# A hybrid decoder layer on one core: the attention's step as two blocks of both heads

## Chip, core and metric

The kernel runs on one NeuronCore of a Trainium2 chip. The metric is the device time of one execution in microseconds (us). An interval or a median is over several executions.

## What is computed

The layer takes `x` of 1024 tokens by 1024 features (float32). Two attentions read projections of the same modulated input: A, a sliding window of 128 tokens with 16 query heads on 2 key heads and a sink logit for each head, and B, three dilations (1, 4, 16) of 8 heads each, joined by the softmax of their log-sums. A feed-forward block follows. Cut to what matters here:

```python
s = jnp.einsum('nbqhgd,nbkhd->nbhgqk', qb, kw, preferred_element_type=jnp.float32) * (dh ** -0.5)
s = jnp.where(mask[None, :, None, None], s, NEG_INF)
m = jnp.max(s, axis=-1)                       # A: also against the sink
p = jnp.exp(s - m[..., None])
denom = jnp.sum(p, axis=-1)                   # A: plus exp(sink - m)
o = jnp.einsum('nbhgqk,nbkhd->nbqhgd', p, vw.astype(jnp.float32))
o = o / denom_t[..., None]
...
merged = jax.nn.sigmoid(ga) * ya + jax.nn.sigmoid(gb) * yb
x = layer_norm(DEEPNORM_ALPHA * x + (1.0 + gate_m) * y, ln1_g[l], ln1_b[l])
```

A block is 128 queries; it sees its own 128 keys and, where the pattern asks for it, the 128 before. A head has 64 features.

## The kernel before

Every float32 product is made of parts: an operand is split into a leading part (`hi`, in a format that TensorE (PE) multiplies in one pass) and the rest (`lo`), and three products are summed: hi*hi, hi*lo, lo*hi. For the weights that is `mac` (lines 130 to 133), for the scores it is done by stacking. A head has only 64 features, so `q_stacks` puts q_hi and q_lo of one head on the two halves of the 128 rows (partitions), and `k_stacks` puts k_hi on both halves: one product of 128 rows gives q_hi*k_hi + q_lo*k_hi. The rest, q_hi*k_lo, is a product of 64 rows. It lies on rows 0 to 63 (`LO`) for head 0 of a pair and on rows 64 to 127 (`HI`) for head 1.

**Units and steps.** A unit is one pair of heads: 12 units of B (4 pairs by 3 dilations), then 8 of A. Each unit has 8 blocks for each of its heads. All blocks but the first see the block before in B's first dilation and in A (products of 256 columns, the first of 128); every other block does in the second dilation; none does in the third. The list `subs` (line 723) cuts a unit into four steps: half 0 with head 0, half 0 with head 1, half 1 with head 0, half 1 with head 1, where a half is four blocks. So a step has four 128-row products (`s<-kh,qs`), then four 64-row products (`s<-kl,qs`), all of one head, all on line 497. They fill two banks of the accumulator (PSUM), two blocks in each; the pool `ps_s` has just these two.

**The rest of a step.** VectorE (DVE) reads each block's scores, scales and masks them into `probs` and takes the maximum (`mx`, line 505); two blocks' maxima are negated into `st` (line 510 or 513). ScalarE (ACT) takes exponentials (line 519). One step later `turn_probs` transposes the blocks on PE into banks `pt` (line 535) and ScalarE copies them to `ptsb` (line 536). After the two steps of a half, `weigh` makes the sums of the values (`po`, line 556), the two heads on the two halves of the output columns.

**What sets the order.** Each engine runs its instructions in program order (`manual_schedule`). The projections are a generator, `stream`, in pieces of six matmuls (a tick); the loop over the steps pumps a number of ticks (`at`) between its parts, so that attention is woven into the projections. A unit of B and the first of A have 24 ticks, the other A units 8. The projections run ahead of the attention by `LEAD = 6` ticks. A unit's query stacks are made two and three ticks behind their projection, head 0 first (`soon`), each by a copy on ScalarE (line 432) and a subtraction on VectorE (line 433). POOL does a part of the rotation; SP issues nearly all DMAs, POOL those of the last A pair's end.

Of the kernel before, what the change touches and what calls it, by code (L numbers as in the profile page):

```python
# [40 lines left out]
class Weights:  # L41
    """Streams weights in pieces of 512 columns: DMA, an optional scale, and two exact parts."""
# [15 lines left out]
    def step(self):  # L58
        """Splits the next piece and sends for the one that fits behind it."""
# [17 lines left out]
    def prepare(self, pieces):  # L77
        """Sees to it that the next pieces are split."""
        while len(self.done) < min(self.used + pieces, len(self.jobs)):
            self.step()  # L80

    def take(self, pieces):
        """The next pieces, as a function from the chunk to its two parts."""
        self.prepare(pieces)
        got = self.done[self.used:self.used + pieces]
        self.used += pieces
        kh = got[0][2]
        n = 512 // kh
        return lambda k: [got[k // kh][s][:, (k % kh) * n:(k % kh + 1) * n] for s in range(2)]
# [3 lines left out]
def decoder_layer(ctx: ExitStack, tc: tile.TileContext, I, out, dbg=None):  # L93
# [20 lines left out]
    # silu(c), one value per partition and chunk of the contraction  # L114
# [6 lines left out]
    def wide(name, pool, halves=(0, 1)):  # L121
        """A [128, 8, 1024] array in two exact parts: a function of part, token half and chunk."""
# [87 lines left out]
    early = {}  # L210
    with tc.tile_pool(name="pro", bufs=2) as pro:
# [52 lines left out]
        def first_macs(j):  # L264
            """What the j-th chunk of u^T brings to the first projections, in pieces."""
# [18 lines left out]
        def table_steps():  # L284
            """The rope's angles, reduced to [-pi, pi] (cosines as sines of a quarter turn less the angle's size)."""
# [141 lines left out]
    def q_stacks(e, r, box):  # L427
        """Per head [q_hi; q_lo], the leading part on the head's own partitions."""
# [13 lines left out]
    def k_stacks(e, r, both, box):  # L442
        """Per head [k_hi; k_hi] and k_lo, on the head's own partitions or on both halves."""
# [21 lines left out]
    def values(e, r, box):  # L465
        """Values [key in block, block, feature], tokens in the order of their residue modulo r."""
# [17 lines left out]
    def scores(un, half, h):  # L484
        """Scaled and masked scores of four blocks of a head, and their maxima, negated."""
        own = (LO, HI)[h]
        box, prev, st = un["box"], un["prev"], un["st"]
        probs = att.tile([P, 4, 2, P], F32, name="probs", bufs=2)
        un["probs", half, h] = probs
        khs, kls = (box["kh"], box["kl"]) if "kv" not in un else ([kv_a["kh"][un["kv"]]] * 2, [kv_a["kl"][un["kv"]]] * 2)  # L490
        q = box["q"][h]
# [8 lines left out]
        mx = att.tile([P, 4], F32, name="mx", bufs=3)  # L500
        for i2 in range(2):
            for j in range(2):
                i = 2 * i2 + j
                lo = 0 if prev(4 * half + i) else 1
                nc.vector.tensor_tensor_reduce(
                    out=probs[:, i, lo:], in0=pss[i2][:, j, lo:], in1=un["mask"][:, lo:], scale=QS, scalar=NEG,
                    op0=OP.add, op1=OP.max, accum_out=mx[:, i:i + 1])
            sl = slice(4 * half + 2 * i2, 4 * half + 2 * i2 + 2)
            if "kv" in un:
                nc.vector.tensor_scalar(st[:, 0, h, sl], mx[:, 2 * i2:2 * i2 + 2], un["sink"](h), -1.0,  # L510
                                        op0=OP.max, op1=OP.mult)
            else:
                nc.vector.tensor_scalar(st[:, 0, h, sl], mx[:, 2 * i2:2 * i2 + 2], -1.0, None, op0=OP.mult)  # L513
    def exponentials(un, half, h):
        prev, st, probs = un["prev"], un["st"], un["probs", half, h]
        for i in range(4):
            b = 4 * half + i
            pr = probs[:, i, 0 if prev(b) else 1:]
            nc.scalar.activation(pr, pr, AF.Exp, bias=st[:, 0, h, b:b + 1], accum_out=st[:, 1, h, b:b + 1])  # L519
    def slots_of(un, half):  # L520
        slots = []
        for b in range(4 * half, 4 * half + 4):
# [5 lines left out]
    def turn_probs(un, half, h):  # L528
        probs, slots = un.pop(("probs", half, h)), slots_of(un, half)
        ptsb = att.tile([P, 8, P], F32, name="ptsb", bufs=3)  # L530
        for s0 in range(0, len(slots), 4):
            part = slots[s0:s0 + 4]
            pt = ps_t.tile([P, 4, P], F32, name="pt")
            for i, (b, kb) in enumerate(part):
                nc.tensor.transpose(pt[:, i, :], probs[:, b - 4 * half, int(kb == b)], ident)  # L535
            nc.scalar.activation(ptsb[:, s0:s0 + len(part), :], pt[:, :len(part), :], AF.Copy)
        un["pts", half, h] = ptsb

    def weigh(un, half):
        """Sums of the values for four blocks of both heads."""  # L540
        slots = slots_of(un, half)
# [7 lines left out]
        pts = [un.pop(("pts", half, h)) for h in range(2)]  # L549
# [3 lines left out]
        for ji, (kb, i, n, c0) in enumerate(jobs):  # L553
            for h in range(2):
                c = un["kv"] if "kv" in un else h
                nc.tensor.matmul(po[(LO, HI)[h], c0:c0 + n * P], v[:, kb, c * 64:(c + 1) * 64], pts[h][:, i:i + n, :],  # L556
# [20 lines left out]
    def keep_sums(un):  # L577
        """The reciprocal sums of A's exponentials, the sinks' among them."""
# [22 lines left out]
    def side(p):  # L601
        """The last pair's end keeps to the engine that has nothing else to do then."""
# [96 lines left out]
    def tasks(n, i):  # L699
        """What follows the attention of earlier units."""  # L700
# [22 lines left out]
    subs = [(un, half, h) for un in units for half in range(2) for h in range(2)]  # L723
    pump(ends[0] + LEAD + 2)
    for s in range(len(subs) + 2):
# [4 lines left out]
        if s < len(subs):  # L730
            un, half, h = subs[s]
            if half == 0 and h == 0:
                un["st"] = att.tile([P, 2, 2, NB], F32, name="st", bufs=3)
            scores(un, half, h)
# [6 lines left out]
        if s >= 2:  # L741
            un, half, h = subs[s - 2]
            if h == 1:
                weigh(un, half)
                if half == 1:
# [436 lines left out]
```

## Time and profile before

| | |
|---|---|
| time, median of 3 runs | 1977.31 us (1974.82 to 1979.35) |
| span of the profiled execution, first to last instruction | 1974.0 us |
| PE / DVE / ACT / POOL busy | 98% / 55% / 34% / 20% |
| attention and its projections | about 88 to 830 us |

The page gives no time of its own for the profiled execution beside its span; the median of the timed runs lies 3.3 us above that span. Matmuls are pipelined and their ends are modelled, so what a matmul costs is read from the distance between starts, not from its duration. `PEld` is the load of the stationary operand, which runs ahead of the products where it can. `PEclk` is the share of TensorE's clock that was granted.

### The profile page before, as it was taken

What the parts mean: (1) busy time and instruction counts of PE and PEld (TensorE: products, weight loads), DVE (VectorE), ACT (ScalarE), POOL (GpSimd) and SP (SyncE); (2) the same over time, 40 slices, a digit from 0 to 9 for tenths busy, and PEclk for the clock granted to TensorE, in tenths of its full rate; (3) what the DMA queues carried; (4) which work ended last, traced back from release to release, by engine and by line L of the source; (5) the groups of instructions that cost most, each with busy time, mean ns of one, the idle gap of its engine ahead of it and who ended that gap; (6) DMA issues with size and microseconds to landing.
All of it is one profiled execution on the core that took longest, in us unless ns stands there. A gap on an engine that the chain in (4) does not pass through costs nothing.

```text
span 1974.0 us, 24286 instructions
## 1 busy us (share of the span) xinstructions
PE 1925.3 (98%) x9252; PEld 1548.0 (78%) x9252; DVE 1088.3 (55%) x2111; ACT 678.5 (34%) x1501; POOL 390.5 (20%) x259
## 2 busy tenths in 40 slices
PE   6899999999999999999999999999999999999998
PEld 5688878878878777778888878787778777877886
DVE  8755567677676877435454558434433343334337
ACT  3555444445445677532121314211121112111222
POOL 2422223323332222001211333000010001000013
PEclk9899999999999999999999999999999999999999
DMA  8011111121121212355442242111111111111112
GB/s 311 22 38 39 36 59 54 39 66 49 34 72 43 89 65 70 126 180 166 160 144 80 62 131 70 54 54 42 39 59 43 43 43 65 38 38 54 54 48 86
DMA packets 68518, 146.16 MB, mean 74 GB/s; under 512 B 12529, under 2 KB 13617, under 8 KB 68402
## 3 DMA queue, kind: packets, MB, share of 16 engines
q1 hardware_dynamic: 68066, 143.56, 22.2%
q8 instruction: 73, 1.20, 0.3%
q0 software_dynamic: 336, 1.06, 0.2%
q14 instruction: 43, 0.35, 0.1%
HBM read 132.69 MB, written 11.89 MB: 73 GB/s over the span
## 4 chain that ended last, share of the span: by engine, by line
PE 84%; DVE 9%; ACT 2%; DMA 2%; issue 2%; POOL 1%; SPq 0%; DVEq 0%; ACTq 0%
PE pf L132 9%; PE pf L131 9%; PE pf L133 9%; PE pj L131 7%; PE pj L133 7%; PE pj L132 7%; PE p L132 5%; PE p L133 5%; PE p L131 5%; PE pd L131 4%; PE pd L133 4%; PE pd L132 4%; PE s L497 3%; PE pt L535 2%; PE po L556 2%
## 5 line engine op out<-in xcount | busy, mean ns | idle before, releaser
L131 PE MATMUL pj<-u,w_hi 128*128 128x512 f32 x720 | 300.8, 418 | 0.0
L73 DVE TENSOR_TENSOR w_lo<-w_raw,w_hi 128x512 fp32r<-128x512 f32 x238 | 198.9, 845 | 174.9 <-ACT w_hi L72 171.8
L133 PE MATMUL pj<-u,w_lo 128*128 128x512 f32 x720 | 283.3, 393 | 0.0
L132 PE MATMUL pj<-u,w_hi 128*128 128x512 f32 x720 | 282.0, 392 | 0.0
L131 PE MATMUL pf<-v,w_hi 128*128 128x512 f32 x704 | 276.5, 393 | 0.0
L132 PE MATMUL pf<-v,w_hi 128*128 128x512 f32 x704 | 276.2, 392 | 0.0
L133 PE MATMUL pf<-v,w_lo 128*128 128x512 f32 x704 | 275.7, 392 | 0.0
L67 POOL TENSOR_TENSOR w_raw<-w_raw,gate 128x512 f32<-128x512 f32 x60 | 81.8, 1369 | 637.6 <-DMA w_raw<-in_w_down 436.2
L418 POOL TENSOR_TENSOR rb<-rb,sin_t 128x512 f32<-128x512 f32 x64 | 86.9, 1357 | 510.3 <-DVE rb L416 359.7
L519 ACT ACTIVATE probs<-probs,st 128x128 f32<-128x128 f32 (+1 forms) x320 | 146.0, 460 | 53.6 <-DVE st L513 26.6
L1096 DVE SCALAR_TENSOR_TENSOR zt<-zt,pd 128x512 f32<-128x512 f32 x160 | 109.3, 688 | 99.4 <-PE pd L133 99.4
L131 PEld LDWEIGHTS pj<-u,w_hi 128*128 128x128 f32 x720 | 135.9, 189 | 33.5 <-issue 4.9
L133 PEld LDWEIGHTS pj<-u,w_lo 128*128 128x128 f32 x720 | 135.5, 188 | 30.7
L1068 ACT ACTIVATE sg<-pf 128x512 f32<-128x512 f32 x44 | 26.3, 597 | 384.2 <-PE pf L133 384.2
L131 PEld LDWEIGHTS pf<-v,w_hi 128*128 128x128 f32 x704 | 131.9, 187 | 30.2
L133 PEld LDWEIGHTS pf<-v,w_lo 128*128 128x128 f32 x704 | 131.9, 187 | 30.2
L72 ACT ACTIVATE w_hi<-w_raw 128x512 fp32r<-128x512 f32 x238 | 144.5, 622 | 32.0 <-PE p L132 12.5
L132 PEld LDWEIGHTS pf<-v,w_hi 128*128 128x128 f32 x704 | 132.0, 187 | 29.8
L132 PEld LDWEIGHTS pj<-u,w_hi 128*128 128x128 f32 x720 | 136.2, 189 | 22.4
L131 PE MATMUL pd<-wd,h 128*128 128x512 f32 x336 | 133.5, 397 | 6.7 <-DVE zt L1096 6.7
L133 PE MATMUL pd<-wd,h 128*128 128x512 f32 x336 | 133.2, 396 | 0.0
L132 PE MATMUL pd<-wd,h 128*128 128x512 f32 x336 | 132.6, 395 | 0.0
(211 smaller groups left out, 3303.8 us busy)
## 6 DMA issues: line engine op xcount, KB each, us to landing
w_raw<-in_w_in SPq DMA_DIRECT2D x118, 256.0 KB
w_raw<-in_w_gate_up SPq DMA_DIRECT2D x88, 256.0 KB
a_raw<-in_w_ada SPq DMA_DIRECT2D x32, 512.0 KB
w_raw<-in_w_down SPq DMA_DIRECT2D x44, 256.0 KB
wa<-in_w_ada_m SPq DMA_DIRECT2D x16, 512.0 KB
wb<-wt_d SPq DMA_DIRECT2D x24, 256.0 KB
xt<-in_xT SPq DMA_DIRECT2D x8, 512.0 KB
w_raw<-in_w_branch_a SPq DMA_DIRECT2D x16, 256.0 KB
```

What stands on the lines that cost most here:

```text
L67: self.nc.gpsimd.tensor_tensor(raw, raw, scale(), op=OP.mult)
L72: self.nc.scalar.activation(hi, raw, AF.Copy)
L73: self.nc.vector.tensor_tensor(lo, raw, hi, op=OP.subtract)
L131: nc.tensor.matmul(ps, w[0], m[0], start=first, stop=False)
L132: nc.tensor.matmul(ps, w[0], m[1], start=False, stop=False)
L133: nc.tensor.matmul(ps, w[1], m[0], start=False, stop=last)
L418: eng.tensor_tensor(b, b, sin_t[:, s], op=OP.mult)
L497: nc.tensor.matmul(pss[i // 2][:, i % 2, lo:], lhs[:, b * P:(b + 1) * P], rhs[:, (b - 1 + lo) * P:(b + 1) * P], start=first and i % 2 == 0 ...
L519: nc.scalar.activation(pr, pr, AF.Exp, bias=st[:, 0, h, b:b + 1], accum_out=st[:, 1, h, b:b + 1])
L535: nc.tensor.transpose(pt[:, i, :], probs[:, b - 4 * half, int(kb == b)], ident)
L556: nc.tensor.matmul(po[(LO, HI)[h], c0:c0 + n * P], v[:, kb, c * 64:(c + 1) * 64], pts[h][:, i:i + n, :], start=(ji == 0), stop=(ji == len( ...
L1096: nc.vector.scalar_tensor_tensor(z, z, ALPHA if gi == 0 else 1.0, pd, op0=OP.mult, op1=OP.add)
```

## The change

The list of steps is cut in another way: a step is two neighbouring blocks of both heads (`qr`, 0 to 3), in place of four blocks of one head. In a step, each head has its own score bank. The 128-row products alternate between the heads, and then the 64-row products alternate between the heads too, and with that between rows 0 to 63 and rows 64 to 127. The maxima, the exponentials and the transposes follow the new order. The turned scores of a half are one buffer of both heads (two buffers of 8 KB in each partition, in place of three of 4 KB); where neither block sees the block before, both heads' four transposes share a bank and one copy. The DMA scratch area, which holds descriptors of POOL's transfers, is set to 2048 bytes in each partition. Comments are dropped throughout.

```diff
-    def scores(un, half, h):
-        own = (LO, HI)[h]
+    def scores(un, qr):
         box, prev, st = un["box"], un["prev"], un["st"]
-        probs = att.tile([P, 4, 2, P], F32, name="probs", bufs=2)
+        probs = att.tile([P, 2, 2, 2, P], F32, name="probs", bufs=2)
...
         pss = [ps_s.tile([P, 2, 2, P], F32, name="s") for _ in range(2)]
-        for lhs, rhs, first in ((q, khs[h], True), (q[own], kls[h][own], False)):
-            for i in range(4):
-                b = 4 * half + i
-                lo = 0 if prev(b) else 1
-                nc.tensor.matmul(pss[i // 2][:, i % 2, lo:], lhs[:, b * P:(b + 1) * P],
-                                 rhs[:, (b - 1 + lo) * P:(b + 1) * P], start=first and i % 2 == 0,
-                                 stop=not first and i % 2 == 1, skip_group_check=True)
+        blocks = [(i, 2 * qr + i, 0 if prev(2 * qr + i) else 1) for i in range(2)]
+        for i, b, lo in blocks:
+            for h in range(2):
+                nc.tensor.matmul(pss[h][:, i, lo:], box["q"][h][:, b * P:(b + 1) * P],
+                                 khs[h][:, (b - 1 + lo) * P:(b + 1) * P], start=i == 0, stop=False,
+                                 skip_group_check=True)
+
+        for i, b, lo in blocks:
+            for h, own in enumerate((LO, HI)):
+                nc.tensor.matmul(pss[h][:, i, lo:], box["q"][h][own, b * P:(b + 1) * P],
+                                 kls[h][own, (b - 1 + lo) * P:(b + 1) * P], start=False, stop=i == 1,
+                                 skip_group_check=True)
...
-    def turn_probs(un, half, h):
-        probs, slots = un.pop(("probs", half, h)), slots_of(un, half)
-        ptsb = att.tile([P, 8, P], F32, name="ptsb", bufs=3)
-        for s0 in range(0, len(slots), 4):
-            part = slots[s0:s0 + 4]
-            pt = ps_t.tile([P, 4, P], F32, name="pt")
+    def turn_probs(un, qr):
+        probs, half = un.pop(("probs", qr)), qr // 2
+        if qr % 2 == 0:
+            un["pts", half] = att.tile([P, 2, 8, P], F32, name="ptsb", bufs=2)
+        ptsb, part = un["pts", half], slots_of(un, 2 * qr, 2 * qr + 2)
+        s0, n = len(slots_of(un, 4 * half, 2 * qr)), len(part)
+        together = 2 * n <= 4
+        for h in range(2):
+            if not (h and together):
+                pt = ps_t.tile([P, 4, P], F32, name="pt")
+            o = n if h and together else 0
             for i, (b, kb) in enumerate(part):
-                nc.tensor.transpose(pt[:, i, :], probs[:, b - 4 * half, int(kb == b)], ident)
-            nc.scalar.activation(ptsb[:, s0:s0 + len(part), :], pt[:, :len(part), :], AF.Copy)
+                nc.tensor.transpose(pt[:, o + i, :], probs[:, h, b - 2 * qr, int(kb == b)], ident)
+            if not together:
+                nc.scalar.activation(ptsb[:, h, s0:s0 + n, :], pt[:, :n, :], AF.Copy)
+        if together:
+            nc.scalar.activation(ptsb[:, :, s0:s0 + n, :], pt[:, :2 * n, :].rearrange("p (h i) q -> p h i q", h=2), AF.Copy)
...
-    subs = [(un, half, h) for un in units for half in range(2) for h in range(2)]
+    subs = [(un, qr) for un in units for qr in range(4)]
...
-    nc = bacc.Bacc("TRN2", target_bir_lowering=False, num_devices=1)
+    nc = bacc.Bacc("TRN2", target_bir_lowering=False, num_devices=1, dynamic_dma_scratch_size=2048)
```

What this does to PE's order is seen at the first step of the first unit. The numbers behind the names tell the buffers apart: `qs_653` and `kh_626` are head 0's stacks, `qs_662` and `kh_637` head 1's, `s_679` and `s_680` the two banks; both heads share the tile `kl_629`, each on its own rows. Before:

```order
L497 MATMUL s_679<-kh_626,qs_653 128x128 [waits DVE_49]
L497 MATMUL s_679<-kh_626,qs_653 128x256
L497 MATMUL s_680<-kh_626,qs_653 128x256 [waits PE_49]
L497 MATMUL s_680<-kh_626,qs_653 128x256
L497 MATMUL s_679<-kl_629,qs_653 128x128
L497 MATMUL s_679<-kl_629,qs_653 128x256
L497 MATMUL s_680<-kl_629,qs_653 128x256 x2
```

And now:

```order
L494 MATMUL s_679<-kh_626,qs_653 128x128 [waits DVE_49,PE_49]
L494 MATMUL s_680<-kh_637,qs_662 128x128 [waits DVE_49,PE_49]
L494 MATMUL s_679<-kh_626,qs_653 128x256
L494 MATMUL s_680<-kh_637,qs_662 128x256
L500 MATMUL s_679<-kl_629,qs_653 128x128
L500 MATMUL s_680<-kl_629,qs_662 128x128
L500 MATMUL s_679<-kl_629,qs_653 128x256
L500 MATMUL s_680<-kl_629,qs_662 128x256
```

The 64-row products (`kl`) now change head and bank each time, and the step's second product waits for VectorE's part of head 1's stack. In the second step, which before was head 1's, the banks `s_745` and `s_746` are waited for. Before:

```order
L497 MATMUL s_745<-kh_637,qs_662 128x128 [waits DVE_49,Activation_49]
L497 MATMUL s_745<-kh_637,qs_662 128x256
L497 MATMUL s_746<-kh_637,qs_662 128x256 [waits DVE_49]
L497 MATMUL s_746<-kh_637,qs_662 128x256
L497 MATMUL s_745<-kl_629,qs_662 128x128
L497 MATMUL s_745<-kl_629,qs_662 128x256
```

And now:

```order
L494 MATMUL s_745<-kh_626,qs_653 128x256 [waits DVE_49]
L494 MATMUL s_746<-kh_637,qs_662 128x256 [waits DVE_49]
L494 MATMUL s_745<-kh_626,qs_653 128x256
L494 MATMUL s_746<-kh_637,qs_662 128x256
L500 MATMUL s_745<-kl_629,qs_653 128x256
```

The wait for the second bank moved from the third product to the second.

## Rows read from the trace of the kernel before

**Rows 1.** The page: busy time of each engine, and the chain by engine.
```profile
PE 1925.3 (98%) x9252; PEld 1548.0 (78%) x9252; DVE 1088.3 (55%) x2111; ACT 678.5 (34%) x1501; POOL 390.5 (20%) x259
...
PE 84%; DVE 9%; ACT 2%; DMA 2%; issue 2%; POOL 1%; SPq 0%; DVEq 0%; ACTq 0%
```

**Rows 2.** Busy time by stretch: start:end, length, each engine's busy time, clock, DMA.
```profile
core 0: us, PE busy (x) PEld busy (x) DVE busy (x) ACT busy (x) POOL busy (x), PEclk, DMA share, GB/s
640.00:700.00 60.00, 57.26 (x339) 43.37 (x339) 52.68 (x149) 40.24 (x113) 11.90 (x10) 1.00 0.25 79
700.00:760.00 60.00, 60.00 (x379) 47.02 (x380) 42.74 (x136) 41.54 (x123) 13.79 (x11) 1.00 0.23 74
900.00:1974.00 1074.00, 1057.27 (x4612) 855.66 (x4610) 494.37 (x691) 213.17 (x369) 162.01 (x107) 1.00 0.21 70
90.90:94.50 3.60, 3.60 (x9) 2.83 (x10) 3.53 (x11) 0.99 (x4) 3.28 (x2) 0.50 0.00 0
```

**Rows 3.** Waits of the weight loader, 85 to 840 us: total, times, longest.
```profile
PEld s L497 <- DVE mx L505: 3.9, 8, 0.8
```

**Rows 4.** Groups of instructions by form: the 64-row products, count, busy us, mean ns.
```profile
L497 PE MATMUL s<-kl,qs 64*128 64x256 f32 x200 | 40.5, 306 | 0.0
...
L497 PE MATMUL s<-kl,qs 64*128 64x128 f32 x120 | 27.1, 290 | 0.0
```

**Rows 5.** Timeline of PE, narrow windows in an A step: start, length, instruction, merged count.
```profile
739.03 0.28 PE L497 MATMUL s<-kh,qs 128*128 128x256 f32 x1
739.23 0.38 PE L497 MATMUL s<-kl,qs 64*128 64x256 f32 x1
739.46 0.40 PE L497 MATMUL s<-kl,qs 64*128 64x256 f32 x2
739.69 0.28 PE L497 MATMUL s<-kl,qs 64*128 64x256 f32 x1
739.90 0.33 PE L535 MATMUL pt<-ident,probs 128*128 128x128 f32 x1
```

**Rows 6.** The same of a step of B's third dilation, second and fourth 64-row product.
```profile
314.31 0.38 PE L497 MATMUL s<-kl,qs 64*128 64x128 f32 x2
314.53 0.27 PE L497 MATMUL s<-kl,qs 64*128 64x128 f32 x1
```

**Rows 7.** Timeline of the weight loader in that step: its four 64-row loads.
```profile
314.14 0.52 PEld L497 LDWEIGHTS s<-kl,qs 64*128 64x128 f32 x4
```

**Rows 8.** Timeline, narrow windows at a `po` group: one and two products, then loads.
```profile
309.34 0.43 PE L556 MATMUL po<-ptsb,v 128*64 128x256 f32 x1
...
309.34 0.44 PE L556 MATMUL po<-ptsb,v 128*64 128x256 f32 x2
...
309.34 0.13 PEld L556 LDWEIGHTS po<-ptsb,v 128*64 128x64 f32 x1 [0.35 <-issue]
309.34 0.14 PEld L556 LDWEIGHTS po<-ptsb,v 128*64 128x64 f32 x2 [0.35 <-issue]
```

**Rows 9.** Timeline at the first unit's first step: VectorE's query stacks, PE's products.
```profile
85.45 4.26 DVE L433 TENSOR_TENSOR qs<-o,qs 64x1024 fp32r<-64x1024 f32 x2
...
88.52 1.23 PE L497 MATMUL s<-kh,qs 128*128 128x128 f32 x4 [6.27 <-DVE qs L433]
```

**Rows 10.** Timeline at unit 5's first step: VectorE's second query stack, PE's first product.
```profile
312.36 1.22 DVE L433 TENSOR_TENSOR qs<-r,qs 64x1024 fp32r<-64x1024 f32 x1
...
313.65 0.22 PE L497 MATMUL s<-kh,qs 128*128 128x128 f32 x1
```

**Rows 11.** Timeline of two A steps: PE's 128-row products, VectorE's last reading.
```profile
668.51 0.50 PE L497 MATMUL s<-kh,qs 128*128 128x256 f32 x2
669.45 0.51 PE L497 MATMUL s<-kh,qs 128*128 128x256 f32 x2 [0.44 <-DVE mx L505]
...
743.61 0.28 PE L497 MATMUL s<-kh,qs 128*128 128x256 f32 x1
...
743.52 0.08 DVE L505 DVE_READ_ACCUMULATOR2_ANT mx<- 128x1 f32 x1
```

More of the change, by code (lines that the diff above doesn't have):

```diff
@@ L482, in values @@
         return project(e, evacuate)
-    def scores(un, half, h):
-        own = (LO, HI)[h]
+    def scores(un, qr):
         box, prev, st = un["box"], un["prev"], un["st"]
-        probs = att.tile([P, 4, 2, P], F32, name="probs", bufs=2)
-        un["probs", half, h] = probs
+        probs = att.tile([P, 2, 2, 2, P], F32, name="probs", bufs=2)
+        un["probs", qr] = probs
         khs, kls = (box["kh"], box["kl"]) if "kv" not in un else ([kv_a["kh"][un["kv"]]] * 2, [kv_a["kl"][un["kv"]]] * 2)
-        q = box["q"][h]
@@ L500, in scores @@
[L500 to L504, printed above, removed]
+        blocks = [(i, 2 * qr + i, 0 if prev(2 * qr + i) else 1) for i in range(2)]
[4 more added lines that the diff above has]
+                                 skip_group_check=True)
@@ L505, in scores @@
+        for i, b, lo in blocks:
[3 more added lines that the diff above has]
+                                 skip_group_check=True)
+        mx = att.tile([P, 2, 2], F32, name="mx", bufs=3)
+        for h in range(2):
+            for i, b, lo in blocks:
                 nc.vector.tensor_tensor_reduce(
-                    out=probs[:, i, lo:], in0=pss[i2][:, j, lo:], in1=un["mask"][:, lo:], scale=QS, scalar=NEG,
@@ L507, in scores @@
[L507 to L508 removed]
+                    out=probs[:, h, i, lo:], in0=pss[h][:, i, lo:], in1=un["mask"][:, lo:], scale=QS, scalar=NEG,
+                    op0=OP.add, op1=OP.max, accum_out=mx[:, h, i:i + 1])
+            sl = slice(2 * qr, 2 * qr + 2)
             if "kv" in un:
[L510 to L513 removed]
@@ L514, in exponentials @@
[L514 to L520, printed above, removed]
+                nc.vector.tensor_scalar(st[:, 0, h, sl], mx[:, h], un["sink"](h), -1.0, op0=OP.max, op1=OP.mult)
+            else:
+                nc.vector.tensor_scalar(st[:, 0, h, sl], mx[:, h], -1.0, None, op0=OP.mult)
@@ L521, in slots_of, with exponentials @@
+    def exponentials(un, qr):
+        prev, st, probs = un["prev"], un["st"], un["probs", qr]
+        for h in range(2):
+            for i in range(2):
+                b = 2 * qr + i
+                pr = probs[:, h, i, 0 if prev(b) else 1:]
+                nc.scalar.activation(pr, pr, AF.Exp, bias=st[:, 0, h, b:b + 1], accum_out=st[:, 1, h, b:b + 1])
+    def slots_of(un, b0, b1):
         slots = []
-        for b in range(4 * half, 4 * half + 4):
+        for b in range(b0, b1):
             if un["prev"](b):
@@ L548, in weigh @@
         po = ps_o.tile([P, TH], F32, name="po")
-        pts = [un.pop(("pts", half, h)) for h in range(2)]
+        pts = un.pop(("pts", half))
         if half == 0:
@@ L555, in weigh @@
                 c = un["kv"] if "kv" in un else h
-                nc.tensor.matmul(po[(LO, HI)[h], c0:c0 + n * P], v[:, kb, c * 64:(c + 1) * 64], pts[h][:, i:i + n, :],
+                nc.tensor.matmul(po[(LO, HI)[h], c0:c0 + n * P], v[:, kb, c * 64:(c + 1) * 64], pts[:, h, i:i + n, :],
                                  start=(ji == 0), stop=(ji == len(jobs) - 1), skip_group_check=True)
@@ L730, in decoder_layer @@
         if s < len(subs):
-            un, half, h = subs[s]
-            if half == 0 and h == 0:
+            un, qr = subs[s]
+            if qr == 0:
                 un["st"] = att.tile([P, 2, 2, NB], F32, name="st", bufs=3)
-            scores(un, half, h)
+            scores(un, qr)
         at(0.4)
@@ L741, in decoder_layer @@
         if s >= 2:
[L742 to L745, printed above, removed]
+            un, qr = subs[s - 2]
+            if qr % 2:
+                weigh(un, qr // 2)
+                if qr == 3:
                     outs[un["a"] if "a" in un else un["b"]] = un["o"]
```

4 lines of the change are left out of this document (2 added, 2 removed).

## Prediction, made before the changed kernel ran

> **What bounds the kernel now.** I read the page first: the tensor engine is busy for 98% of the span, and the chain that ended last lies on it for 84% [rows 1]. Since a matmul's end is modelled, I then took the table of busy time by stage: in the attention (700 to 760 us as a sample) and behind 900 us it is full or nearly so, and VectorE and ScalarE have room [rows 2]. Only between 640 and 700 us, where the last B pair is joined while the A units run, does it stand still for 2.7 of 60 us, and there VectorE is busy for 52.7 us [rows 2]. The waits of the weight loader say for what: for VectorE's readings of the score banks (`mx`), eight times, 3.9 us in all [rows 3]. So a microsecond less on the tensor engine is nearly a microsecond less of the span wherever PE doesn't wait, and that must be read step by step.
>
> A step's own cost comes from the timeline of one A step. The four 64-row products (`kl`) run on one half of the rows: the first one's load starts at 739.23, the second product starts at 739.46, the fourth at 739.69, and the next work (of 128 rows again) at 739.90 [rows 5]. So two gaps take 0.23 us, 0.115 us each, with 256 columns; the 0.23 ahead of the second holds the exposed first load; the 0.21 behind the fourth is the drain before the rows' mode changes. With 128 columns two gaps take 314.53 - 314.31 = 0.22 us, 0.11 each [rows 6], which is the pace of the loads: four of them take 0.52 us, the last 0.19 of it, so (0.52 - 0.19) / 3 = 0.11 us apart [rows 6, 7].
>
> **What the change removes.** The 320 64-row products stay 320 (200 of 256 columns, 120 of 128 [rows 4]), but they now come as 160 neighbours of equal width, one on rows 0 to 63 with its bank and one on rows 64 to 127 with the other bank. If the halves work side by side, each pair costs one gap instead of two: 100 x 0.115 + 60 x 0.11 = 18.1 us. Whether they do, no row of before shows for row halves, as the halves never meet in one step there. The nearest row is the sum of the values (`po`), whose neighbours lie on the two column halves: one product of 256 columns lasts 0.43 us by the record, two together 0.44, and the two loads, of which one alone lasts 0.13 to 0.14 us, 0.14 [rows 8]. There both loads and both products run side by side, and the second costs about 0.01 us. I carry that over to row halves. The bounds: 18.1 us gained at one end; 48 us lost at the other (the third rival), if a change of half cost what a change of mode costs.
>
> The Trainium skill's "TensorEngine Tiling (Array Packing)" (Key Properties) says that a change of tiling mode drains the engine while a change of tile doesn't, and that tiles load and multiply independently. The drain agrees with the 0.21 us above; for row tiles no run so far shows it. By that rule the term would be these same 18.1 us.
>
> **What stays.** The number of steps (80), their changes between 128 and 64 rows, the transposes, VectorE's readings and ScalarE's exponentials are the same in number and size. ScalarE's copies of the turned scores go from 512 + 256 columns to twice 384 in the second dilation, as many copies of as many columns in all: nothing. In that dilation the 128-row products come as 128, 128, 256, 256 columns, not alternating; the pace of such a batch lies between the 0.11 and 0.115 above with some of the alternation's unevenness gone; I take 0.5 us off over its 16 steps, with 0 and 1 us as bounds. The buffers of turned scores (three of a head, now two of both heads) are asked for one half later than they come free, so nobody waits. POOL's and SP's queues have the same order. The smaller DMA scratch touches only POOL's few transfers at the attention's end; I cost it at nothing, as their data is wanted by the second branch projection alone; if that cover were gone, the price would be one transfer, a few us.
>
> **What it adds: waits.** (a) Step 0 of a unit now needs both heads' query stacks, where before the second was needed a step later. In the first unit PE already waits 6.27 us for the first stack and starts at 88.52; VectorE ends the second at 85.45 + 4.26 = 89.71 [rows 9]. Only the first product can go ahead: 1.2 us later, less the part of the batch already done; I take 1.0. Queued behind it are all of PE's projections, and VectorE's readings of that step. The granted clock is 0.50 there (1.2 GHz, after the idle time) as late as 94.5 [rows 2]; if it stays low for another such stretch of 3.6 us, that is 1.8 us more, the upper bound; the lower bound is 0.5. In units 5, 8 and 11 the second stack ends at 312.36 + 1.22 = 313.58 and step 0 starts at 313.65 [rows 10], with 0.2 us less PE work between them: about 0.1 each, 0.3 together. Elsewhere the stacks are ready well ahead.
> (b) The second 128-row product now needs the second score bank; before, two products came ahead of that wait. At 668.51 two products run and the third starts only at 669.45, 0.44 us of it idle [rows 11]: in such a step one product less lies ahead of the wait, 0.115 us. The loader's eight waits [rows 3] lie in six steps between 644 and 697 us: 0.7 us.
> (c) In those steps the end is set by ScalarE and VectorE (exponentials, then the query stacks, then the readings), which don't get faster, so PE's gain there becomes a longer wait. Of nine steps in that stretch I write off seven: 7 x 0.23 = 1.6 us. In four A units behind it, the step before each unit's last is tight: VectorE ends its last reading at 743.60, and the third product, which needs it, starts about 0.23 behind 743.61 [rows 11]; as second product it would come at 743.73, and 0.23 earlier by the gain: a wait of 0.1 each, 0.4 us together.
>
> **The sum**: -18.1 - 0.5 + 1.0 + 0.3 + 0.7 + 1.6 + 0.4 = -14.6 us. The profiled execution's span is 1974.0 us, so 1959.4; the median of the three runs shown is 1977.3, 3.3 us above that span, and the same 14.6 us off it give 1962.7.
>
> **The rivals.**
> 1. *The A units swallow their part.* Their 32 steps hold 8 pairs of 128 and 56 of 256 columns, 7.3 of the 18.1 us. If the chain over ScalarE and VectorE decides in all of them, not in nine steps, B's 10.8 us remain, less 1.3 for (a) and 32 x 0.115 = 3.7 for (b), plus the 0.5: -6.3, so 1971. For it: the 0.1 us of slack above. Against it: from 700 us on PE shows no idle time at all, with VectorE at 42.7 of 60 us [rows 2]. The Trainium skill's tiling page (PSUM Bottleneck) warns of this: tiling speeds up TensorE but not the evacuation of its banks; the stretch at 640 to 700 agrees, the one behind it not.
> 2. *The change doesn't do what it says: products overlap but loads don't.* Four loads 0.11 apart [rows 7] then set the pace of every step, as they do now with 128 columns. The wider pairs gain at most 100 x (0.115 x 2 - 0.11 x 2) = 1 us, and (a) and (b) cost 2.0: 1977 to 1979. For it: loads are already the limit at 128 columns, and row halves may share one path. Against it: the two loads of `po` within 0.14 us [rows 8].
> 3. *Slower: a change of half drains like a change of mode.* From the last 128-row product's start (739.03) to the second 64-row one's (739.46) it takes 0.43 us [rows 5], 0.20 more than two plain gaps. With three changes of half in each of 80 steps: 240 x 0.20 = 48 us, less nothing: about 2025. It decides if the second half's load can't start before the first half's product has ended. For it: the records show such a drain at every change between 64 and 128 rows. Against it: no drain between column halves [rows 8].
>
> **How the numbers follow.** Forecast as summed, 0.64; its own range is 1957 (all of (a) to (c) hidden, -18.6, and runs scatter by about 2 us) to 1967. First rival 0.14 (1967 to 1972), second 0.15, third 0.05, and 0.02 for a still larger gain. The range from 1957 to 1972 holds the forecast and the first rival, just under 8 in 10. A change under 0.2% (4 us) can't be told from none. Faster by more than that: 0.64 + 0.14 + 0.02 = 0.80; within: the second rival, 0.15; slower: 0.05.
>
> **What would show it.** In the timeline after, the four `kl` products of a step should start as two twins, and from the first load to the next mode's load it should take 0.43 us, not 0.67 (0.37, not 0.59, with 128 columns). A batch still 0.6 us long speaks for the second rival, one of 1.2 us for the third. PE's wait ahead of the first unit's second product should be 1.2 us, and the waits for `mx` between 644 and 697 us should grow by 1 to 2 us, with few new ones behind 700. If new waits for `mx` or for `probs` appear in every A unit, the first rival is right. The forecast is wrong if the twins are there and yet the span behind the attention starts less than 10 us earlier.

## The result, and the profile after

| | before | after |
|---|---|---|
| median of 4 runs each | 1977.44 us (1974.82 to 1979.35) | 1964.61 us (1962.28 to 1966.63) |
| span of the profiled execution | 1974.0 us | 1962.5 us |
| ratio after / before, 95% interval | | 0.9939 (0.9924 to 0.9953) |

The change takes 12.8 us off the median. The two profiled spans are 11.5 us apart; the difference of 1.3 us is scatter: all executions that list both lie 1.8 to 2.1 us above their span, so the profiled execution of before was a run of about 1976, a little under its median.

The page after, its engines and its chain of work by engine, answers to [rows 1]:

```profile
PE 1908.2 (97%) x9252; PEld 1529.0 (78%) x9252; DVE 1083.1 (55%) x2111; ACT 678.4 (35%) x1501; POOL 390.8 (20%) x259
...
PE 82%; DVE 10%; ACT 3%; DMA 2%; issue 2%; POOL 1%; SPq 0%; DVEq 0%; ACTq 0%
```

As many instructions as before on every engine. PE is busy for 17.1 us less, and the span is shorter by 11.5: about a third of what PE saves comes back as waiting. The chain says on whom: VectorE and ScalarE have a point each more. The groups of the 64-row products by form (count, busy time, mean ns), as in [rows 4]:

```profile
L500 PE MATMUL s<-kl,qs 64*128 64x256 f32 x200 | 27.7, 332 | 0.0
...
L500 PE MATMUL s<-kl,qs 64*128 64x128 f32 x120 | 16.3, 312 | 0.0
```

The same 200 and 120 products, each lasting as long as before or longer (306 and 290 ns in [rows 4]), occupy PE for 44.0 us together, not 67.6: they lie on top of each other. (That is time in which a 64-row product is in flight; what the path gained is in the ledger below.) How, the timeline of PE shows in four narrow windows of an A step (start, length, instruction, how many were merged), to be held against [rows 5]:

```profile
753.53 0.28 PE L494 MATMUL s<-kh,qs 128*128 128x256 f32 x1
753.73 0.39 PE L500 MATMUL s<-kl,qs 64*128 64x256 f32 x2
...
753.96 0.28 PE L500 MATMUL s<-kl,qs 64*128 64x256 f32 x2
754.17 0.33 PE L543 MATMUL pt<-ident,probs 128*128 128x128 f32 x1
```

Two twins, at 753.73 and at 753.96, each two products merged into one row no longer than one of them. In the trace the second of a pair starts 3 or 4 ns behind the first (753.733 and 753.737, then 753.957 and 753.960). From the batch's start to the next mode it takes 0.44 us, where [rows 5] had 0.67. The loads run side by side too: this batch's four take 0.30 us in all, where the four of [rows 7], all on one half, took 0.52:

```profile
753.73 0.30 PEld L500 LDWEIGHTS s<-kl,qs 64*128 64x128 f32 x4
```

Waits of PE between 85 and 840 us (total, times, longest), of the kernel before and then of the one after, and the loader's wait of [rows 3] after:

```profile
PE pt L473 <- ACT vt L477: 2.5, 3, 0.8
PE s L497 <- DVE mx L505: 2.0, 4, 0.6
PE pt L570 <- ACT ptsb L536: 0.8, 3, 0.3
```

```profile
PE s L494 <- DVE qs L433: 7.2, 2, 6.3
PE s L494 <- DVE mx L506: 3.9, 10, 1.1
PE pt L473 <- ACT vt L477: 2.8, 3, 0.9
PE pt L580 <- ACT ptsb L545: 2.6, 3, 0.9
...
PEld s L494 <- DVE mx L506: 8.0, 14, 1.2
```

Three waits grew most. For the readings `mx` PE stands 3.9 us in ten places, not 2.0 in four. For the second query stack of the first unit 0.8 us came on top of the 6.3. And in three places, line 580, PE waits for `ptsb` for 2.6 us instead of 0.8 (line 580 is what was 570: the transpose in `send_stats`). This third one the prediction did not have. The stretches of [rows 2] (start:end, length, busy time of each engine, granted clock, DMA):

```profile
640.00:700.00 60.00, 55.95 (x347) 41.34 (x346) 49.57 (x142) 40.03 (x118) 11.75 (x10) 1.00 0.28 86
700.00:760.00 60.00, 59.46 (x385) 45.58 (x384) 44.60 (x140) 43.25 (x124) 12.87 (x10) 1.00 0.21 67
900.00:1962.50 1062.50, 1046.14 (x4564) 846.68 (x4562) 479.58 (x678) 211.67 (x366) 158.94 (x105) 1.00 0.21 69
```

Between 640 and 700 us PE now stands still for 4.0 us instead of 2.7, and from 700 to 760, where it showed no idle time, for 0.5 us. Behind 900 us nothing changed: 16.4 us idle of 1062.5, before 16.7 of 1074.0.

### The ledger

The first 128-row product of each of the 80 steps marks the step's start; the differences of these starts, and of the starts inside a step, give each term its measured size. The first row sums the batches of 64-row products; each other row is what the steps that it names changed by beside that:

| term | forecast, us | measured, us |
|---|---|---|
| 160 pairs of 64-row products | -18.1 | -18.3 |
| order of the 128-row products, second dilation | -0.5 | 0.0 |
| (a) first unit waits for its second stack | +1.0 | +1.0 |
| (a) units 5, 8, 11 | +0.3 | +0.5 (0.17 each) |
| (b) and (c), units 12 to 14 | +2.3 | +2.6 |
| (c) A units 15 to 18 | +0.4 | +1.7 (0.45 at each last step, a little less elsewhere) |
| second steps of units 4, 7, 10 | not seen | +2.2 (0.74 each) |
| sum (of the unrounded values) | -14.6 | -10.2 |

The last step's start moved by 10.2 us (it lies at 805.63). Behind it another 1.2 us come off the span (1158.1 us from there to the end before, 1156.9 after), of which 0.7 lie in the branch projections' wait for `o_hl` (2.7 us before, 2.0 after). Neither is shown to be the change's doing: over the ten profiled executions of this document that stretch, whose work is the same in all, lasts 1153.3 to 1158.1 us, and the wait 1.7 to 2.9. So much of the scatter lies behind the attention, and the steps' starts are a finer ruler than the medians.

### The profile page after: what moved, and what is told of

The parts are those of the page before. It is cut to its first block, busy times and chain, and to the rows that moved or that the text cites. A ratio compares the mean times of both kernels' runs of the same rounds, so it can differ in the third digit from the quotient of the medians.

```text
span 1962.5 us, 24309 instructions
## 1 busy us (share of the span) xinstructions
PE 1908.2 (97%) x9252; PEld 1529.0 (78%) x9252; DVE 1083.1 (55%) x2111; ACT 678.4 (35%) x1501; POOL 390.8 (20%) x259
## 4 chain that ended last, share of the span: by engine, by line
PE 82%; DVE 10%; ACT 3%; DMA 2%; issue 2%; POOL 1%; SPq 0%; DVEq 0%; ACTq 0%
PE pf L132 9%; PE pf L131 9%; PE pf L133 9%; PE pj L131 7%; PE pj L133 6%; PE pj L132 6%; PE p L132 5%; PE p L133 5%; PE p L131 5%; PE pd L131 4%; PE pd L133 4%; PE pd L132 4%; PE pt L543 2%; PE po L566 2%; PE s L494 1%
## 5 line engine op out<-in xcount | busy, mean ns | idle before, releaser
L72 ACT ACTIVATE w_hi<-w_raw 128x512 fp32r<-128x512 f32 x238 | 144.5, 622 | 31.9 <-PE p L132 12.5
```

The lines of the kernel that those rows point to most:

```text
L72: self.nc.scalar.activation(hi, raw, AF.Copy)
```

## Experiments

The kernel before was run beside each batch: 1976.07 us in the first (e1 to e4), 1976.37 in the second (e5 to e8). All edits are against the changed kernel unless said otherwise.

### Is it the neighbours? The 64-row products by head (e1)

```diff
-        for i, b, lo in blocks:
-            for h, own in enumerate((LO, HI)):
+        for h, own in enumerate((LO, HI)):
+            for i, b, lo in blocks:
```

> The changed kernel (1964.6 us) with one thing undone: the four 64-row products of a step go head by head (both blocks on rows 0 to 63, then both on rows 64 to 127), no longer alternating. Theory (neighbours on different halves of the rows run side by side, all others come one gap apart): only the two in the middle still overlap, so a batch takes 0.55 us in place of 0.43 (0.48 in place of 0.37 with 128 columns): 80 x 0.11 = 9 us more on the tensor engine, of which some 3 come back as shorter waits: 1970 to 1972 us. Rival A (a twin must stand first in its group, so nothing overlaps here): batches of 0.66 us, 1976 to 1979. Rival B (the gain came from the new order of the steps, not from the two halves): batches as before the change and the time at 1964 to 1966.

Measured: 1963.07 us (1961.38 to 1964.48, 5 runs), ratio 0.9933 (0.992 to 0.9945). Undoing the alternation costs nothing, and the time I expected is wrong. The batches are as short as in the changed kernel (0.43 us, 0.37 with 128 columns). Where the two blocks of a step differ in width, the records even say in which order PE ran them. The program now has 128 and 256 columns on rows 0 to 63, then 128 and 256 on rows 64 to 127. Three narrow windows of PE's timeline at such a step of e1 (the first ends between the first two starts):

```profile
133.22 0.33 PE L500 MATMUL s<-kl,qs 64*128 64x128 f32 x1
...
133.22 0.33 PE L500 MATMUL s<-kl,qs 64*128 64x128 f32 x2
...
133.38 0.34 PE L500 MATMUL s<-kl,qs 64*128 64x256 f32 x2
```

Both products of 128 columns start together (7 ns apart in the trace), and 0.16 us later both of 256: 128, 128, 256, 256, where the program says 128, 256, 128, 256. The third product overtook the second, which started 0.16 us behind the first of its own half. So it is in all 28 steps of unequal widths, and the built program has the written order, so the engine made the pairs. Here the product of the other half stood one place further on in its queue; the order written in the loop does not matter. What the change needs is both halves in one step.

### Is it the halves at all? All four on one half (e5)

Head 1's product runs on rows 0 to 63 as well, so its q_hi*k_lo is left out and its q_lo is multiplied in its place; number and size of the products stay.

```diff
-            for h, own in enumerate((LO, HI)):
+            for h, own in enumerate((LO, LO)):
```

> The changed kernel (1964.6 us) with both heads' 64-row products on rows 0 to 63, in the same order as in the changed kernel (head 1's product then takes other numbers than its own: the part q_hi*k_lo of head 1 is left out). Theory (the two halves of the rows make the gain, whatever the order): no twins, batches of 0.66 us (0.59 with 128 columns) as before the change, 18 us more on the tensor engine, of which 3 to 5 come back as shorter waits: 1977 to 1980. Rival (the gain lies in the order of the steps, the banks or the heads' alternation): twins or batches of 0.43 us stay, 1964 to 1966.

Measured: 1975.35 us (12 runs), ratio 0.9995 (0.9986 to 1.0003): no difference from the kernel before. The median is 1.7 us below the range that I expected, within the scatter of its runs (1972.49 to 1981.19). Summed over the 80 steps, the batches last 0.09 us more than before (0.665 us each in the wide steps, again). This run has everything else of the change, the order of steps, heads and banks, the buffers and the DMA scratch, so none of these makes the gain. By itself the new cut of steps costs the first unit's wait of 1.0 us, of which 0.4 come back in the same unit, and 0.3 us in units 12 to 14; small gains elsewhere leave 0.4 us over all steps. The second steps of units 4, 7 and 10 last 14.53 to 14.55 us, before 14.50, and the A units 15 to 18 keep their steps to within 0.1 us. So the ledger's losses in these units are made by the gain, not by the new order.

### Who holds PE in units 4, 7 and 10? The joining left out (e4)

In the unit behind each joined B pair, `combine_weights` works out the three dilations' weights on VectorE with 16 rows. Here it keeps its transfers alone; the arithmetic between them is left out.

```diff
     def combine_weights(p):
...
-        nc.vector.tensor_tensor(nat(nmx, 4), nat(st[:, 0, 0], 4), tok(st[:, 1, 0], 4), op=OP.min)
...
-        nc.scalar.activation(st[:, :, 0], st[:, :, 0], AF.Exp)
...
-        nc.vector.reciprocal(tot, tot)
```

> The changed kernel (1964.6 us) without the arithmetic that joins the three dilations' weights (the function combine_weights keeps its loads and stores and leaves out everything between them), about 8 us of VectorE and one ScalarE instruction for each of the four B pairs. Theory: the second step of units 4, 7 and 10, which got 0.5 us longer with the change, not 0.23 shorter, is held by this block: VectorE reads the scores late, the next key stack comes late, ScalarE is blocked behind it, and the tensor engine waits for two banks to be copied. Without the block these waits (5.4 us in three units) go, and some of those in units 12 and 13: 1958 to 1960. Rival: ScalarE's own queue holds these banks: the waits stay and the time is 1963 to 1965.

Measured: 1957.63 us (1955.92 to 1960.26, 4 runs), ratio 0.9906 (0.9893 to 0.992). The second steps of units 4, 7 and 10 take 12.93 us each instead of 15.01, 2.07 less, 6.2 together; the last step starts 6.1 us earlier. That agrees, and both waits in these steps (`pt L473` and `pt L580`) are gone from the list. The chain itself is read from two timelines. Unit 4 in the kernel after, VectorE's first joining instruction, its first reading of the scores that PE had ready at 264.7, ScalarE's first key stack, its copy of the turned scores, and PE's product that waits for it (in brackets the idle time before and its releaser):

```profile
262.30 0.36 DVE L636 TENSOR_TENSOR cst<-cst 16x128 f32<-16x128 f32 x1
...
271.16 0.27 DVE L506 CUSTOM_DVE_ANT_0 probs<-s,mask 128x128 f32<-128x128 f32 x1
...
277.49 1.06 ACT L447 ACTIVATE kh<-r 64x1024 fp32r<-64x1024 f32 x1 [3.54 <-POOL r L419]
...
283.49 0.85 ACT L545 ACTIVATE ptsb<-pt 128x384 f32<-128x384 f32 x2
...
284.02 0.29 PE L580 MATMUL pt<-ident,st 128*32 128x128 f32 x1 [0.88 <-ACT ptsb L545]
```

The same places in the kernel before:

```profile
264.96 0.37 DVE L626 TENSOR_TENSOR cst<-cst 16x128 f32<-16x128 f32 x1
...
280.13 1.06 ACT L447 ACTIVATE kh<-r 64x1024 fp32r<-64x1024 f32 x1 [3.55 <-POOL r L419]
...
286.14 0.85 ACT L536 ACTIVATE ptsb<-pt 128x512 f32<-128x512 f32 x2
...
286.77 0.28 PE L570 MATMUL pt<-ident,st 128*32 128x128 f32 x1 [0.25 <-ACT ptsb L536]
```

From the joining's start to the copy it takes 283.49 - 262.30 = 21.19 us after and 286.14 - 264.96 = 21.18 before: a chain over VectorE (8 us of joining, the readings and the projection's turn queued behind), POOL and ScalarE that no twin shortens. PE arrives 0.6 us earlier and waits 0.88 instead of 0.25. The joining's own start gains nothing either: in both kernels it lies 10.74 us behind the start of unit 3's last step (251.56 after, 254.22 before). So three steps' gain falls into this chain, 0.26, 0.24 and 0.22 us, and 0.74 are lost. This is the mechanism of the first rival, but in B units, where the prediction had not looked.

### The same, with all work kept: the joining cut in two (e6), and before with the cut (e8)

`combine_weights` is run in two parts, minima, differences and exponentials one step earlier, the rest where it was:

```diff
-    def combine_weights(p):
+    def combine_weights(p, part):
...
+        if part == 0:
...
+            return
...
-        if "b" in last and last["b"][1] == 2 and i == 3:
-            combine_weights(last["b"][0])
+        if "b" in last and last["b"][1] == 2 and i >= 2:
+            combine_weights(last["b"][0], i - 2)
```

> The changed kernel (1964.6 us) with the arithmetic that joins the dilations cut in two: maxima, differences and exponentials (4.4 us of VectorE) one step earlier, the rest where it was. Theory: the second steps of units 4, 7 and 10 are held by this block on VectorE; with 4.4 us of it moved into a step where VectorE idles, they lose their waits (2.07 us each when the whole block was left out): 6 us less, 1958 to 1960. Rival: the first part now delays the query stacks of units 4, 7 and 10, whose first steps then wait: less than 2 us gained, 1963 to 1965.

Measured: 1959.59 us (1958.58 to 1962.08, 4 runs), ratio 0.9914 (0.9902 to 0.9927). As expected. The three steps shrink from 15.01 to 13.37 us. VectorE's first joining instruction in that step of e6 and its first reading there:

```profile
263.35 0.53 DVE L644 TENSOR_TENSOR cst<-cst 16x384 f32<-16x384 f32 x1
...
269.87 0.27 DVE L506 CUSTOM_DVE_ANT_0 probs<-s,mask 128x128 f32<-128x128 f32 x1
```

The reading comes 6.5 us behind the joining's start, not 8.9. Of the 4.9 us gained in these three steps, 1.2 are lost again in units 12 to 14, where PE's waits for `mx` grow once more; from the first step to the last 3.8 remain. Each run of this kernel is faster than each of the changed kernel, though the two ratios' intervals overlap a little (0.9924 to 0.9927).

The same cut in the kernel before:

> The kernel before (1976.1 us in the last comparison) with the joining arithmetic cut in two, and nothing else. The change lost 0.74 us in each of the three second steps (0.51 longer, not 0.23 shorter), which were held by VectorE already. Theory: before the change these steps wait about 1.1 us each, so the cut gives 3.3 us here and about 6 in the changed kernel: 1972 to 1973.5; the twins' gain, measured between the two cut kernels, is then about 15 us, not 12. Rival: no wait to speak of before the change: within 1 us of 1976.

Measured: 1973.2 us (1971.19 to 1975.58, 11 runs), ratio 0.9984 (0.9976 to 0.9993). By the medians the cut is worth about 3.2 us without the twins (1.4 to 4.7 by the interval) and, by the two medians' distance from their runs of before (16.8 against 12.8), about 4 with them. From the first step's start to the last's it is 1.8 and 3.8. The three steps fall by 1.35 us each here, but 1.5 us of the 4.0 are lost again in units 12 to 14, and 0.8 in the first unit, where nothing was cut. Between the two cut kernels the last step starts 12.5 us apart, where it was 10.2 between the uncut ones: more of the twins' gain arrives, but not the 15 that I expected. Without the twins the three steps take 13.15 us, as long as the second step of unit 1, which has no joining (13.15), and their waits are gone from the list: the chain no longer sets their end. With the twins they take 13.37, where unit 1's takes 12.93: there the chain, even cut, still costs 0.44 us each.

### The order of the 128-row products (e2)

```diff
-        for i, b, lo in blocks:
-            for h in range(2):
+        for h in range(2):
+            for i, b, lo in blocks:
```

> The changed kernel (1964.6 us) with the four 128-row products of a step head by head again (both blocks of head 0, then both of head 1); the 64-row products still alternate. So the second score bank and the second head's query stack are wanted by the third product, not the second. Theory: one more product, 0.115 us, runs ahead of every such wait: about ten A steps, units 5, 8 and 11 and, at half the clock, the first step: 1.5 to 2 us less, 1962.6 to 1963.1. Rival: the products that go ahead only lengthen the wait behind them, since the last product after the wait sets the batch's end either way: no change within 0.5 us.

Measured: 1963.78 us (1960.91 to 1964.08, 5 runs), ratio 0.993 (0.9917 to 0.9944). Both products of head 0 now go ahead of the wait for the second bank and the second stack, and the batches of 128-row products get 1.8 us shorter in sum (0.2 in the first unit, 0.5 in the rest of B, 0.7 in units 12 to 14, 0.4 in units 15 to 18). That is the price of wanting the second bank and the second stack one product sooner, (b) and a part of (a), with the sign that was expected; of it 1.3 us arrive in the steps. The median is only 0.8 us below the changed kernel's, outside the range that I expected and too close to tell from nothing.

Together with the cut joining (e7):

> The changed kernel (1964.6 us) with both: the 128-row products head by head, and the joining arithmetic cut in two. Theory: these lie in different steps, so they add: 6 us of the cut and 1.3 of the order, 1956.5 to 1958.5. Rival: the waits are shared, and the sum is that of the cut alone, 1958 to 1960.

Measured: 1961.14 us (1958.83 to 1961.88, 5 runs), ratio 0.9915 (0.9903 to 0.9928): by the median no better than e6 alone, against my expectation. In the steps it is better. From the first start to the last it saves 4.3 us against the changed kernel, where e6 saves 3.8 and e2 1.3: most of the sum. Its batches of 128-row products are 1.9 us shorter than those of e6, its steps only 0.6; in units 12 to 14 the batches get 0.8 us shorter, and what follows them in these steps 0.7 longer. Why the median doesn't show the 0.6 us stays open. In the two profiled executions the stretch behind the last step is 2.5 us longer in e7 (1157.2 against 1154.7), inside the scatter told above, and PE's waits in the branch projections, of e6 and then of e7, are 0.7 us of it:

```profile
PE p L132 <- DVE o_hl L112: 1.3, 2, 0.9
PE p L131 <- ACT o_hl L111: 0.4, 1, 0.4
```

```profile
PE p L131 <- ACT o_hl L111: 1.4, 1, 1.4
PE p L132 <- DVE o_hl L112: 1.0, 1, 1.0
```

These waits lie between 1.7 and 2.9 us in the ten profiled executions, so this one pair does not make them the cause.

### Later query stacks in the A units (e3)

In units 15 to 18 PE waits 0.45 us at the last step. If ScalarE's and VectorE's stack work ahead of the reading does it, the second stack one place later in the queues must take the wait away:

```diff
-                soon(2 + h + (4 if e < EARLY else 0), lambda h=h: stack(res, h))
+                soon(2 + h + (4 if e < EARLY else 0) + (h if e > 36 else 0), lambda h=h: stack(res, h))
```

> The changed kernel (1964.6 us) with the second query stack of the A units 1 to 7 made a tick later, so that it stands behind the readings and the exponentials of the step in its way, not ahead of them. Theory: the 0.45 us waits ahead of the last step of units 15 to 18 end a chain over ScalarE and VectorE that begins when the query projection ends and goes through both query stacks; with 1.06 + 1.22 us out of it these waits go (1.8 us) and some of those in units 13 and 14 too (1 to 2 us): 1961 to 1962.5. Rival: the wait is set by VectorE's readings and ScalarE's exponentials themselves, whose number did not change: still 0.4 us in each of these steps, 1964 to 1965.

Measured: 1970.54 us (1969.64 to 1971.49, 6 runs), ratio 0.9971 (0.996 to 0.9983): 6 us slower than the changed kernel. Of the two things said, the first is right: in these units PE's first batch gets 1.79 us shorter in sum, which is four times 0.45. But the copy of the stack now stands ahead of the copy of the turned scores. ScalarE and PE at unit 16's last step in e3:

```profile
741.30 1.05 ACT L432 ACTIVATE qs<-r 64x1024 fp32r<-64x1024 f32 x1
742.38 0.60 ACT L545 ACTIVATE ptsb<-pt 128x512 f32<-128x512 f32 x1
...
743.03 0.66 PE L543 MATMUL pt<-ident,probs 128*128 128x128 f32 x4 [0.84 <-ACT ptsb L545]
```

Such waits come to 5.6 us in six places, and one for `sr` is new; the largest losses, 2.3 and 3.0 us, are in the first two steps of unit 13:

```profile
PE pt L543 <- ACT ptsb L545: 5.6, 6, 1.5
...
PE pt L543 <- DVE sr L602: 1.8, 1, 1.8
```

The stack work is the cause, and moving it by one place only moves the wait. What sets the 0.45 us is read from the two timelines. Unit 17 after, from the second step's first product over ScalarE's and VectorE's query stacks to the end of the last reading and PE's product behind it:

```profile
746.57 0.28 PE L494 MATMUL s<-kh,qs 128*128 128x256 f32 x1
...
751.90 1.04 ACT L432 ACTIVATE qs<-r 64x1024 fp32r<-64x1024 f32 x1
...
755.45 1.22 DVE L433 TENSOR_TENSOR qs<-r,qs 64x1024 fp32r<-64x1024 f32 x1 [0.21 <-ACT qs L432]
...
758.32 0.08 DVE L506 DVE_READ_ACCUMULATOR2_ANT mx<- 128x1 f32 x1
...
758.45 0.62 PE L494 MATMUL s<-kh,qs 128*128 128x256 f32 x3 [0.18 <-DVE mx L506]
```

And before:

```profile
755.33 0.39 PE L497 MATMUL s<-kh,qs 128*128 128x128 f32 x2
...
760.67 1.04 ACT L432 ACTIVATE qs<-r 64x1024 fp32r<-64x1024 f32 x1
...
764.21 1.22 DVE L433 TENSOR_TENSOR qs<-r,qs 64x1024 fp32r<-64x1024 f32 x1 [0.20 <-ACT qs L432]
...
767.08 0.08 DVE L505 DVE_READ_ACCUMULATOR2_ANT mx<- 128x1 f32 x1
```

From the second step's first product to the end of the last reading it takes 758.40 - 746.57 = 11.83 us after and 767.16 - 755.33 = 11.83 before. In that time lie two of PE's steps, and the gain of both, 0.46 us, is lost but for the slack that was there.

## Why the prediction was right, and where not

**The main term.** The pairs gave 18.3 us for the 18.1 summed; e5 shows that they are all of the gain. The reading behind it, that `po`'s neighbours on the two column halves [rows 8] stand for row halves too, held: the second product of a pair starts 3 or 4 ns behind the first, and the batch has the 0.43 us (0.37 with 128 columns) that was to be looked for. The second rival needed loads that follow each other 0.11 us apart (four now take 0.30 us, not 0.52), the third a drain at each change of half; neither is there. The rule of the Trainium skill's "TensorEngine Tiling (Array Packing)" (Key Properties) that tiles load and multiply in parallel agrees here also for row tiles.

**The waits.** (a) in the first unit was 1.0 us for 1.0: the wait for the second stack is 0.80 us and the product before it goes ahead alone. VectorE's stacks there, and PE's first products, as in [rows 9]:

```profile
85.23 4.26 DVE L433 TENSOR_TENSOR qs<-o,qs 64x1024 fp32r<-64x1024 f32 x2
...
88.39 0.45 PE L494 MATMUL s<-kh,qs 128*128 128x128 f32 x1 [6.35 <-DVE qs L433]
89.64 0.98 PE L494 MATMUL s<-kh,qs 128*128 128x128 f32 x3 [0.80 <-DVE qs L433]
```

The distance of the first two starts is 1.25 us. The low clock ended a little later, not another 3.6 us: in the stretch from 94 to 96 us the granted clock (the third column from the end) is 0.64 after, and 0.81 in the row of before under it. With 0.50 (1.2 GHz) and 1.00 (2.4 GHz) as the two levels, that is 1.44 and 0.76 us of these two at the lower one. It was not longer in all: from 84 to 86 us, before the first product, the clock is 0.80 after and 0.63 before, so it also began about 0.7 us later.

```profile
94.00:96.00 2.00, 2.00 (x7) 1.62 (x6) 0.45 (x1) 1.51 (x5) 0.43 (x1) 0.64 0.00 0
```

```profile
94.00:96.00 2.00, 2.00 (x9) 1.61 (x8) 0.67 (x1) 1.30 (x5) 0.64 (x1) 0.81 0.00 0
```

(a) in units 5, 8 and 11 was 0.17 each for 0.1, and (b) with (c) in units 12 to 14 was 2.6 for 2.3. PE's waits for `mx` between 644 and 697 us were to grow by 1 to 2 us; in the stretch from 640 to 700 they went from 2.0 to 3.1. Behind it there are four new ones, 0.7 us, one in each of units 15 to 18.

**What was mis-sized.** The term of 0.4 us for the four A units was 1.7. I took the reading's end as fixed against the step just before it, so that one step's 0.23 us less the slack was lost. The chain that ends in that reading starts a step earlier, so that PE's gain of two steps runs into it. The slack that I had read from [rows 11] was right (743.73 - 743.60 = 0.13 us); the point from which to count was not: 0.46 - 0.13 = 0.33, and the second product comes 0.34 us late. Another 0.1 us, which I had no term for, is lost behind the wait, where the third product follows 0.22 us behind the second and not 0.12. The 0.5 us for the order in the second dilation were nothing, the bound of that term.

**What was missed.** "Elsewhere the stacks are ready well ahead" was said of the query stacks, and that PE does not wait elsewhere was taken from one stretch between 700 and 760 us and one list of the loader's waits for `mx`. The list of waits of before already had PE standing in units 4, 7 and 10, 2.5 us at `pt L473` and 0.8 at `pt L570`. A step in which PE waits for a chain of other engines does not pass a gain on. Three such steps cost 0.74 us each: their own gain of 0.22, and that of the two steps before, which fall into the same chain. With the joining out of the way (e4) or cut (e6, e8) the steps get shorter by 2.07, 1.64 and 1.35 us.

In the steps forecast and outcome differ by 4.4 us: 1.3 and 2.2 for these two terms, and 0.9 over the smaller ones. The median came closer, 1964.6 for 1962.7, because 1.2 us more went behind the attention and the profiled execution of before lay 1.3 under its median. Both are within the scatter of these measures, and that is luck. By its own sign, a span behind the attention that starts 10 us earlier, the forecast held narrowly: the last step starts 10.2 us earlier.

The first rival, that all A units swallow their part, did not come true, but there is a part of it in the outcome: of the 7.1 us that the eight A units gain in batches of 64-row products up to the last step, 2.8 stay, where my sum had left 4.4. Its sign, new waits for `mx` in every A unit, came in units 15 to 18. Units 12 to 14, where PE waited before the change already, give back nearly all of their 2.8 us; from unit 15 on 2.7 of 4.3 stay.

## What to carry to other kernels

Where products fill only half of the rows, put work of both halves into the same stretch of the queue: in this kernel 320 products cost what 160 do. The two products of a pair write to different banks in every run here; whether they also run side by side in one bank is not shown. Before summing such a gain, list for every repeated place where the engine waits at all, whatever the amount, and follow that chain back to its start: every gain between that start and the wait runs into it, not only that of the last step, and what exceeds the slack is lost. The next thing to do is then at the late chain, and there cutting one long piece of work of another engine (e6: 1959.59 us, ratio 0.9914 (0.9902 to 0.9927) to the kernel before, faster than it and than the changed kernel by their medians) was worth about 4 us more (3.8 in the steps). And where the scatter lies in a part that didn't change, compare the starts inside the trace, not the medians alone.

## What was not expected of the hardware

PE started matmuls of one half of the rows ahead of earlier ones of the other half: in e1 the starts are 133.215, 133.222, 133.379 and 133.385 us for 128, 128, 256 and 256 columns, written as 128, 256, 128, 256. The rows tell the size and not the half, but the sizes leave only one assignment. The Trainium skill's "TensorE: Matmul & The Clock Gate" (Part 3, The mechanism) has matmuls start and end strictly in program order; this trace disagrees for the start, and the measurement decides. How far ahead a product may be taken from the queue, no run here shows; it was one place.
